# A two-layer hybrid block on one core: the second layer's compression issued earlier, the last layer norm on PSUM sums, the overflow branch behind the stores

## The chip, the cores and the metric

The kernel runs on one core of a Trainium2 chip. The metric is the device time of one execution in microseconds; three runs are given, and their median counts. The engines are called as in the profile: PE (TensorE matmuls), PEld (TensorE weight loads), DVE (VectorE), ACT (ScalarE), POOL (GpSimd), SP (SyncE, which here issues nearly all DMA transfers).

## The reference

256 tokens of width 1024 in float32 go through two layers. Layer 1 has a mixer of differential and sparse attention and a dense feed-forward net; layer 2 has a mixer of block attention and a compressed-and-selected attention (NSA), and a mixture of 8 experts with 2 experts for each token. Every part is followed by a layer norm of `alpha * x + part`:

```python
x = layer_norm(DN_ALPHA * x + mix, ln_mix_g[l], ln_mix_b[l])
ffn = moe_swiglu(x, w_router, b_router, w_gate, w_up, w_down)   # layer 2
x = layer_norm(DN_ALPHA * x + ffn, ln_ffn_g[l], ln_ffn_b[l])
```

The compression of NSA takes blocks of 32 tokens (stride 16), adds a position term, and puts each through a small net to get one compressed key and one value per block:

```python
h = moveaxis(blocks + pe, 3, 2).reshape(B, Nc, G, L * dh)
return gelu(h @ phi_w1) @ phi_w2
```

## The kernel before

**Stages.** Layer 1's attention runs until about 150 us, its feed-forward net until about 340, layer 2's attention until about 500, the experts until about 1366, and the last layer norm to the end. Products in float32 precision are made of three passes over split operands: ACT casts a weight tile `raw` to `wh`, DVE subtracts to get `wl` (lines 150 and 152), and PE multiplies (lines 164 to 166). All weight tiles are 128x1024 float32 (512 KB), loaded by SP in program order into a ring of `raw` tiles; a load waits until the tile's former content has been used.

**Layer 2's attention.** The projections of the normed input are made by `project()`, each from four weight tiles (three for the 280 columns of `c_w`): first kv (`c_kv`), then dq, then w, ckB, cq and cv. Names that come up below: `kvc`, the projected kv rows; `kp`, their regrouping on PE by 16 small products (L710); `km`, ACT's copy of it; `xr`, eight DVE copies into the order of the compression (L721); `hp`, 32 products with the eight phi tiles that SP loads (L729, L731); `cmp_hs`, DVE's copy of it; `ht`, the sum over four groups (L737); `cmp_u`, the gelu; `kc` and `vc`, the compressed keys and values. All of this is `compress()`, and stands in the program behind the w projection. `router_weights()` (L854 to L862) turns the layer norm's rows into the router's weights on PE (`rtps`, `rsps`), DVE and ACT (`rowT`, `gwr`) and stands ahead of the w projection. `compressed()` makes the scores against the compressed keys. The softmaxes are those of `softmax8` (L364 the mask product `sps`, L369 the maximum, L372 the exponentials `e`).

A scheduler moves instructions within each engine's order where it expects them to fit; in the experts PE's order is that of the program.

**Experts.** Each expert's 3584 columns are taken in chunks of 1024; experts with few tokens use 64 slots (`gate_up_small`, `down_small`): `pgu` (L1124), activation `h_s`, its transpose `tps` (L1151), the copy `hT_s`, and `y` (L1169). When an expert is done, `combine` scales `y` by the gate, splits it in two parts `yh` (ACT) and `yl` (DVE), multiplies both by the transposed dispatch matrix into a bank `cps` of PSUM (L1191, L1192), and DVE adds that bank to the sum `acc` (here named `x`) in SBUF (L1196), once for each of two token tiles t and two halves c.

**The end.** Slots can be too few for the tokens. A flag `overi` is therefore read by every engine (L1245), and each engine branches on it (L1249) over a long piece of code that computes such tokens. With these inputs the flag is zero and the piece is jumped over. Behind it stand the loads of the last layer norm's rows g and b (L224, L225, on SP), the statistics (L233), the reciprocal root (L206 to L214, for each of two token tiles with its own instructions), the normalising steps on DVE (L242, L244) for t=0 and on ACT, POOL and DVE for t=1 (L1265 to L1267), and four stores (L1269).

Of the kernel before, what the change touches and what calls it, by code (L numbers as in the profile page):

```python
# [8 lines left out]
F32 = mybir.dt.float32  # L9
F32R = mybir.dt.float32r  # L10
# [7 lines left out]
P = 128  # L18
S = 256
D = 1024  # L20
# [19 lines left out]
def hybrid_kernel(ctx, tc, x, ev_w_in, ev_w_out, dif_lambda, dif_subln, ffd_w_gate, ffd_w_up, ffd_w_down,  # L40
# [56 lines left out]
    colrow = const.tile([P, P], F32, name="colrow")  # L97
# [3 lines left out]
    identb = const.tile([P, P], BF16, name="identb")  # L101
    nc.vector.tensor_copy(identb, ident)
    causalb = const.tile([P, P], BF16, name="causalb")
    nc.vector.tensor_scalar(causalb, colrow, 0.0, NEG, op0=ALU.is_gt, op1=ALU.mult)

    loads = []
# [594 lines left out]
            nc.vector.tensor_tensor(fold[r], ident[r, q * 32:q * 32 + 30],  # L701
                                    ident[r, q * 32 + 30:q * 32 + 31].to_broadcast([32, 30]), ALU.add)

    def compress():
        kp = bank((P, 2, 2, P), "kp")
        for z in range(2):
            for g in range(2):
# [10 lines left out]
        for z in range(2):  # L718
            for g in range(2):
                for jj in range(2):  # L720
                    nc.vector.tensor_copy(  # L721
                        xr[:, z, 8 * jj:8 * jj + 8, g * NCMP:(g + 1) * NCMP],
                        km[:, z, g].rearrange("p (n j) -> p j n", j=8)[:, :, jj:jj + NCMP])
        hp = bank((P, 2, S), "hp")
        for z in range(2):
            for q in range(4):
# [178 lines left out]

    rbank = bank
    project(xp, w1[:, 2048:2560], 512, c_kv, None, (normed[-2],) * 3 + (normed[-1],))
    project(xp, w1[:, 1536:2048], 512, c_dq)
    router_weights()
    project(xp, w1[:, 2560:2840], 280, c_w)  # L910
    compress()
    ec = compressed()
    project(xp, w1[:, 512:1024], 512, c_rope(to_blocks, ckB, False))
    os_ = [nsa_start(qt) for qt in range(NT)]
    project(xp, w1[:, 0:512], 512, c_rope(to_heads, cqT, True))
    project(xp, w1[:, 1024:1536], 512, lambda t, ps: nc.scalar.copy(cv[:, t], ps))
# [78 lines left out]
    nc.vector.tensor_scalar(overi, over, 0.49, None, op0=ALU.add)  # L995

    acc = x3

    def columns(r):
        return (posm[:, :, 0:1], weight[:, :, 0:1]) if r is None else (posr[:, :, r:r + 1], weightr[:, :, r:r + 1])  # L1000
# [197 lines left out]
    def experts(runs, groups, small, disp):  # L1198

        turns, pend = [], []  # L1200

        def mid():
            while turns:
                turns.pop(0)()

        for p, (r, base) in enumerate(runs):
            if r is None:
                e = 0
            else:
                with behind(loads[-1] if p else None):  # L1210
                    e = nc.values_load(idxi[0:1, r:r + 1], engines=(mybir.EngineType.SP,), min_val=1, max_val=NE - 1)
            ws = weights_of(e)
            sm = r in small
            xe, gs, dT = disp.pop((r, base))
            ys = [yp.tile([P, 512], F32, tag="y", name="y") for _ in range(1 if sm else 2)]
            for i, (c0, n) in enumerate(CHUNKS):
                hs = (gate_up_small if sm else gate_up)(ws, c0, n, xe, mid)
                for f in pend:
                    f()
                ts = []  # L1220
                turns.append(lambda ts=ts, hs=hs, sm=sm: ts.extend((turn_small if sm else turn)(hs)))
                pend = [lambda ws=ws, c0=c0, n=n, ts=ts, ys=ys, sm=sm: (down_small if sm else down)(ws, c0, n, ts, ys)]
# [6 lines left out]
            pend.append(lambda ys=ys, gs=gs, dT=dT, p=p: turns.append(  # L1229
                lambda: combine(ys, gs, dT, p == 0 and bool(small))))  # L1230
        mid()
        for f in pend:
            f()
        mid()

    disp = dispatch_small(None, True)
    for t in range(NT):
# [2 lines left out]
        with tc.issue_after(marks["d"]):  # L1240
            nc.vector.tensor_tensor(xl[:, t], x3[:, t], xh[:, t].bitcast(F32), ALU.subtract)
    with products_in_order():
        experts([(r, 0) for r in ORDER], {0: ((1,),), 1: ((2, 4), (3,)), 3: ((5,), (6,)), 5: ((7,),)}, FEW, disp)
    def tokens_over(i):
        return nc.values_load(overi[0:1, i:i + 1], min_val=0, max_val=S)  # L1245

# [2 lines left out]
    with tc.If(any_over > 0):  # L1249
        for i, run in enumerate(MORE):  # L1250
            with tc.If(tokens_over(i + 1) > 0):
                experts([run], {}, (), dispatch([run]))

    g, b = ln_rows(1, 1, nc.sync, raw_tile)
    for t in (1, 0):
        z = acc[:, t]
        mu, r = layer_stats(z)
        cs = [slice(h * 512, (h + 1) * 512) for h in range(2)]
        if t == 0:
            normalize(z, mu, r, g, b, z)  # L1260
        else:
            mr = act.tile([P, 1], F32, tag="ln_mr", name="ln_mr", bufs=2)
            nc.vector.scalar_tensor_tensor(mr, mu, -1.0, r, op0=ALU.mult, op1=ALU.mult)  # L1263
            for c, eng in zip(cs, (nc.gpsimd, nc.vector)):
                nc.scalar.activation(z[:, c], z[:, c], AF.Identity, bias=mr, scale=r)  # L1265
                eng.tensor_tensor(z[:, c], z[:, c], g[:, c], ALU.mult)  # L1266
                eng.tensor_tensor(z[:, c], z[:, c], b[:, c], ALU.add)  # L1267
        for c in cs:
            nc.sync.dma_start(out[0, t * P:(t + 1) * P, c], z[:, c])  # L1269


_INS = ['x', 'ev_w_in', 'ev_w_out', 'dif_lambda', 'dif_subln', 'ffd_w_gate', 'ffd_w_up', 'ffd_w_down',
# [35 lines left out]
```

## Time and profile before

| | |
|---|---|
| three runs | 1387.89, 1393.18, 1397.38 us |
| median | 1393.18 us |
| profiled execution, its own time | 1393.63 us |
| its span in the profile | 1391.9 us |
| mean granted TensorE clock | 0.96 |
| PE busy | 1306.8 us (94%) |
| DVE busy | 753.0 us (54%) |
| ACT busy | 543.4 us (39%) |
| DMA, mean over the span | 309 GB/s |

Busy shares are means over stages that differ: in the experts' stage the DMA engines are busy nearly all the time, in the attention PE is, and at the end none is. Idle time counts only where nothing else runs on the engine that everything waits for. Rows of the trace follow below, in a section of their own.

### The profile page before, as it was taken

What the parts mean: (1) busy time and instruction counts of PE and PEld (TensorE: products, weight loads), DVE (VectorE), ACT (ScalarE), POOL (GpSimd) and SP (SyncE); (2) the same over time, 40 slices, a digit from 0 to 9 for tenths busy, and PEclk for the clock granted to TensorE, in tenths of its full rate; (3) what the DMA queues carried; (4) which work ended last, traced back from release to release, by engine and by line L of the source; (5) the groups of instructions that cost most, each with busy time, mean ns of one, the idle gap of its engine ahead of it and who ended that gap; (6) DMA issues with size and microseconds to landing.
All of it is one profiled execution on the core that took longest, in us unless ns stands there. A gap on an engine that the chain in (4) does not pass through costs nothing. (4 is left out here: it accounts for less than half of the span.)

```text
span 1391.9 us, 18210 instructions
## 1 busy us (share of the span) xinstructions
PE 1306.8 (94%) x6136; PEld 851.5 (61%) x6136; DVE 753.0 (54%) x1194; ACT 543.4 (39%) x796; POOL 48.9 (4%) x79
## 2 busy tenths in 40 slices
PE   8979999998988989998999999999999999999992
PEld 7856888886864763335367874546885436885430
DVE  6987755547578551111178963137994127894304
ACT  4464444432446310001066751135773025773100
POOL 2200000001220000000000000000000000000000
PEclk9999999999999979998999999899999999999996
DMA  9244646545553399899999999899999999999992
GB/s 351 73 136 137 227 144 219 182 122 164 175 153 121 126 358 401 340 409 409 402 409 408 402 409 403 320 408 409 407 405 380 409 401 409 409 402 409 408 402 99
DMA packets 146805, 429.98 MB, mean 309 GB/s; under 512 B 15696, under 2 KB 23280, under 8 KB 146704
## 3 DMA queue, kind: packets, MB, share of 16 engines
q1 hardware_dynamic: 146000, 426.48, 80.7%
q0 software_dynamic: 704, 2.26, 0.6%
q8 instruction: 50, 0.82, 0.2%
q14 instruction: 51, 0.42, 0.1%
HBM read 427.64 MB, written 1.05 MB: 308 GB/s over the span
## 5 line engine op out<-in xcount | busy, mean ns | idle before, releaser
L152 DVE TENSOR_TENSOR wl<-raw,wh 128x1024 fp32r<-128x1024 f32 x378 | 453.5, 1224 | 101.7 <-ACT wh L150 94.1
L150 ACT CAST wh<-raw 128x1024 fp32r<-128x1024 f32 x378 | 388.3, 1047 | 201.8 <-PE pg L166 48.7
L1124 PE MATMUL pgu<-raw,xs 128*64 128x512 f32 x1120 | 260.9, 614 | 0.0
L1124 PEld LDWEIGHTS pgu<-raw,xs 128*64 128x64 f32 x1120 | 80.9, 141 | 155.3 <-issue 141.9
L1169 PE MATMUL y<-raw,hT_s 128*64 128x512 f32 x560 | 127.6, 595 | 5.1 <-DMA raw<-in_moe_w_down_dram 3.5
L1132 DVE TENSOR_TENSOR h_s<-h_s,pgu 64x512 f32<-64x512 f32 x35 | 24.1, 690 | 177.8 <-ACT h_s L1131 177.7
L1131 ACT ACTIVATE h_s<-pgu 64x512 f32<-64x512 f32 x35 | 20.7, 590 | 187.0 <-PE pgu L1124 187.0
L1169 PEld LDWEIGHTS y<-raw,hT_s 128*64 128x64 f32 x560 | 38.6, 137 | 88.3 <-issue 67.2
L164 PE MATMUL mmps<-wh,xTh 128*128 128x512 f32 (+2 forms) x192 | 76.4, 399 | 1.0 <-ACT wh L150 0.8
L166 PE MATMUL mmps<-wh,xTl 128*128 128x512 f32 (+2 forms) x192 | 75.6, 395 | 1.8 <-DVE xTl L173 1.7
L165 PE MATMUL mmps<-wl,xTh 128*128 128x512 f32 (+2 forms) x192 | 74.2, 388 | 0.5 <-DVE wl L152 0.5
L164 PE MATMUL y<-wh,hTh 128*128 128x512 f32 x168 | 67.6, 402 | 5.0 <-ACT wh L150 5.0
L164 PE MATMUL pg<-wh,xeh 128*128 128x512 f32 x168 | 70.4, 419 | 0.4
L165 PE MATMUL pg<-wl,xeh 128*128 128x512 f32 x168 | 68.3, 407 | 2.3 <-DVE wl L152 2.3
L165 PE MATMUL y<-wl,hTh 128*128 128x512 f32 x168 | 67.4, 401 | 2.3 <-DVE wl L152 2.3
L166 PE MATMUL pg<-wh,xel 128*128 128x512 f32 x168 | 67.9, 404 | 0.0
L166 PE MATMUL y<-wh,hTl 128*128 128x512 f32 x168 | 67.2, 400 | 0.0
L166 PE MATMUL pu<-wh,xel 128*128 128x512 f32 x168 | 66.3, 395 | 0.0
L165 PE MATMUL pu<-wl,xeh 128*128 128x512 f32 x168 | 66.1, 394 | 0.0
L164 PE MATMUL pu<-wh,xeh 128*128 128x512 f32 x168 | 65.8, 392 | 0.0
L327 DVE COPY hT_s<-tps 128x256 f32<-128x256 f32 x18 | 7.6, 424 | 91.6 <-PE tps L1151 91.5
L325 ACT COPY hT_s<-tps 128x256 f32<-128x256 f32 x17 | 6.3, 372 | 114.6 <-PE tps L1151 114.6
(376 smaller groups left out, 1929.9 us busy)
## 6 DMA issues: line engine op xcount, KB each, us to landing
raw<-in_moe_w_up_dram SPq DMA_DIRECT2D x224, 512.0 KB, 10.1
raw<-in_moe_w_gate_dram SPq DMA_DIRECT2D x224, 512.0 KB, 10.1
raw<-in_moe_w_down_dram SPq DMA_DIRECT2D x224, 512.0 KB, 10.1
raw<-in_ffd_w_gate_dram SPq DMA_DIRECT2D x22, 512.0 KB, 4.9
raw<-in_ffd_w_up_dram SPq DMA_DIRECT2D x22, 512.0 KB, 4.5
raw<-in_ffd_w_down_dram SPq DMA_DIRECT2D x22, 512.0 KB, 4.8
raw<-in_ev_w_in_dram SPq DMA_DIRECT2D x20, 512.0 KB, 8.9
raw<-in_od_w_in_dram SPq DMA_DIRECT2D x20, 512.0 KB, 4.2
```

The source lines that it names most:

```text
L150: nc.scalar.copy(wh[:, :w], rv)
L152: nc.vector.tensor_tensor(wl[:, :w], rv, wh[:, :w].bitcast(F32), ALU.subtract)
L164: nc.tensor.matmul(ps, ah, wh, start=first and i == 0, stop=False)
L165: nc.tensor.matmul(ps, ah, wl, start=False, stop=False)
L166: nc.tensor.matmul(ps, al, wh, start=False, stop=last and i == n - 1)
L325: nc.scalar.copy(dst, src)
L327: nc.vector.tensor_copy(dst, src)
L1124: nc.tensor.matmul(p_[i * SMALL:(i + 1) * SMALL], xs[:, k0 + k], halves(w[k], n)[j], start=k0 + k == 0, stop=k0 + k == KD - 1)
L1131: nc.scalar.activation(h[:SMALL], p_[:SMALL], AF.Silu)
L1132: nc.vector.tensor_tensor(h[:SMALL], h[:SMALL], p_[SMALL:], ALU.mult)
L1169: nc.tensor.matmul(ys[0][i * SMALL:(i + 1) * SMALL], ts[k], w[:, i * 512:(i + 1) * 512], start=c0 == 0 and k == 0, stop=c0 + n == F_EXP an ...
```

## The change

It has three parts.

1. `compress()` is split. `compress_rows()` holds kp, km and xr and is called right behind the kv projection; `compress(xr)` holds the phi loads and all that follows and is called behind the dq projection, ahead of the w projection. `router_weights()` moves from ahead of the w projection to behind it, and `compressed()` from ahead of the ckB projection to behind it.
2. The last expert's combination is summed in PSUM. `residual()` splits the sum `acc` of the experts before into two parts `ah` and `al` and multiplies them by a unit matrix (`identr`) into four banks `zps` ahead of the last `y` products; `combine_last` adds the last expert to these banks. The last layer norm takes its statistics from the banks, has one reciprocal root of width 2 for both token tiles, normalises t=1 on ACT and DVE and t=0 on DVE, and GpSimd has no part in it. The loads of g and b stand behind the last weight load.
3. The branch on `overi` stands behind the four stores. If it is not jumped over, `acc` (copied back by ACT) is completed, normed and stored again.

Three small constants (`colrow`, `identb`, `causalb`) also move to a pool that is freed before the experts.

```diff
-    def compress():
+    def compress_rows():
         kp = bank((P, 2, 2, P), "kp")
...
+        return xr
+
+    def compress(xr):
         hp = bank((P, 2, S), "hp")
...
     project(xp, w1[:, 2048:2560], 512, c_kv, None, (normed[-2],) * 3 + (normed[-1],))
+    xr = compress_rows()
     project(xp, w1[:, 1536:2048], 512, c_dq)
+    compress(xr)
+    project(xp, w1[:, 2560:2840], 280, c_w)
     router_weights()
-    project(xp, w1[:, 2560:2840], 280, c_w)
-    compress()
+    project(xp, w1[:, 512:1024], 512, c_rope(to_blocks, ckB, False))
     ec = compressed()
-    project(xp, w1[:, 512:1024], 512, c_rope(to_blocks, ckB, False))
...
+    def residual():
+        zs = []
+        for t in range(NT):
+            ah = wsplit.tile([P, D], F32R, tag="wh", name="ah")
+            al = wsplit.tile([P, D], F32R, tag="wl", name="al")
+            nc.scalar.copy(ah, acc[:, t])
+            nc.vector.tensor_tensor(al, acc[:, t], ah.bitcast(F32), ALU.subtract)
+            zs.append([gu.tile([P, 512], F32, tag="gu", name="zps") for _ in range(2)])
+            for part in (ah, al):
+                for c in range(2):
+                    nc.tensor.matmul(zs[t][c], identr, part[:, c * 512:(c + 1) * 512], start=part is ah, stop=False)
+        return zs
+
+    def combine_last(zs, ys, gs, dT):
+        yh, yl = split_y(ys[0], gs)
+        for part in (yh, yl):
+            for t in (1, 0):
+                for c in range(2):
+                    rows = slice(c * SMALL, (c + 1) * SMALL)
+                    nc.tensor.matmul(zs[t][c], dT[rows, t], part[rows], start=False, stop=part is yl)
...
         mid()
+        zs = residual() if last else None
         for f in pend:
             f()
         mid()
+        if last:
+            combine_last(zs, ys, gs, dT)
+        return zs
...
+    g, b = ln_rows(1, 1, nc.sync, raw_tile)
+    x4 = [raw_tile() for _ in range(NT)]
...
+    for t in (1, 0):
+        for c in range(2):
+            nc.vector.bn_stats(st[:, t, c], zs[t][c])
+        nc.vector.bn_aggr(mv[:, t], st[:, t].rearrange("p a b -> p (a b)"))
+    r = rsqrt(mp, mv[:, :, 1], 1.0, EPS, NT)
+    mr = mp.tile([P, 1], F32, name="last_mr")
+    ready = nc.vector.scalar_tensor_tensor(mr, mv[:, 1, 0:1], -1.0, r[:, 1:2], op0=ALU.mult, op1=ALU.mult)
+    cs = [slice(c * 512, (c + 1) * 512) for c in range(2)]
+    for c in range(2):
+        nc.scalar.activation(x4[1][:, cs[c]], zs[1][c], AF.Identity, bias=mr, scale=r[:, 1:2])
+    with behind(ready.ins):
+        for c in range(2):
+            z = x4[0][:, cs[c]]
+            nc.vector.scalar_tensor_tensor(z, zs[0][c], mv[:, 0, 0:1], g[:, cs[c]], op0=ALU.subtract, op1=ALU.mult)
+            nc.vector.scalar_tensor_tensor(z, z, r[:, 0:1], b[:, cs[c]], op0=ALU.mult, op1=ALU.add)
+            nc.sync.dma_start(out[0, 0:P, cs[c]], z)
+
+    for t in range(NT):
+        for c in range(2):
+            nc.scalar.copy(acc[:, t, cs[c]], zs[t][c])
+    for c in range(2):
+        z = x4[1][:, cs[c]]
+        nc.vector.tensor_tensor(z, z, g[:, cs[c]], ALU.mult)
+        nc.vector.tensor_tensor(z, z, b[:, cs[c]], ALU.add)
+        nc.sync.dma_start(out[0, P:2 * P, cs[c]], z)
+
     def tokens_over(i):
...
-    g, b = ln_rows(1, 1, nc.sync, raw_tile)
-    for t in (1, 0):
-        z = acc[:, t]
-        mu, r = layer_stats(z)
...
+        g, b = ln_rows(1, 1, nc.sync, raw_tile)
+        for t in range(NT):
+            layer_norm(acc[:, t], g, b)
+            nc.sync.dma_start(out[0, t * P:(t + 1) * P], acc[:, t])
```

The first place is layer 2's attention, on SP. The listing is the order of DMA issues, minus for before and plus for after; `od_w_in` are the projections' weights, `nsa_phi_w` the phi tiles.

```order
 L131 DMA raw<-in_od_w_in_dram 128x2x512 x8
+L733 DMA raw<-in_nsa_phi_w_dram 128x4x256 x8
 L131 DMA raw<-in_od_w_in_dram 128x3x280 x2
 L131 DMA raw<-in_od_w_in_dram 128x2x280
-L729 DMA raw<-in_nsa_phi_w_dram 128x4x256 x8
-L131 DMA raw<-in_od_w_in_dram 128x2x512 x8
```

The eight phi loads now stand ahead of the three loads of the w projection, and the loads for ckB and cq still behind both.

The second place is PE in the same stage. Before, the rows around hp and ht, behind the products of the ckB projection, which the scheduler had put ahead of them:

```order
L165 MATMUL mmps<-wl,xTh 128x512
L166 MATMUL mmps<-wh,xTl 128x512
L731 MATMUL hp<-raw,xr 32x256 x32
L737 MATMUL ht<-fold,cmp_hs 128x30 x4
L164 MATMUL mmps<-wh,xTh 128x512
```

After the change, the rows around hp, at the end of the dq projection; `hps` are the transposes of dq's rows, and the products of 280 columns are those of w:

```order
L164 MATMUL mmps<-wh,xTh 128x512
L333 MATMUL hps<-ident,roped 128x128 x4
L165 MATMUL mmps<-wl,xTh 128x512
L166 MATMUL mmps<-wh,xTl 128x512
L735 MATMUL hp<-raw,xr 32x256 x5
L333 MATMUL hps<-ident,roped 128x128 x4
L735 MATMUL hp<-raw,xr 32x256 x12
L333 MATMUL hps<-ident,roped 128x128 x4
L735 MATMUL hp<-raw,xr 32x256 x15
L164 MATMUL mmps<-wh,xTh 128x280
```

hp and ht stood next to each other; now hp stands between dq and w, and ht (L741) inside the w projection.

The third place is the end of SP's order. Before, from the last weight load on; the code that the branch jumps over is left out:

```order
L131 DMA raw<-in_moe_w_down_dram 128x1024
L1245 TENSOR_LOAD overi
L1245 ISA x2
L1249 COMPARE_AND_BRANCH
...
L224 DMA raw<-in_ln_ffn_g_dram 128x1024
L225 DMA raw<-in_ln_ffn_b_dram 128x1024
L1269 DMA out_dram<-x_2897 128x512 x4
```

And after the change:

```order
L131 DMA raw<-in_moe_w_down_dram 128x1024
L1310 TENSOR_LOAD overi
L1310 ISA x2
L224 DMA raw<-in_ln_ffn_g_dram 128x1024
L225 DMA raw<-in_ln_ffn_b_dram 128x1024
L1298 DMA out_dram<-raw 128x512 x2
L1307 DMA out_dram<-raw 128x512 x2
L1314 COMPARE_AND_BRANCH
```

The loads of g and b no longer stand behind the branch, and the branch stands behind the stores.

## Rows read from the trace of the kernel before

**Rows 1.** Busy time by stretches of the span. Columns: stretch in us and its length; busy us and number of instructions of PE, PEld, DVE, ACT and POOL; granted TensorE clock (1.00 is full speed); busy share of the 16 DMA engines; GB/s.

```profile
340.00:500.00 160.00, 149.28 (x875) 110.90 (x875) 107.91 (x258) 67.78 (x169) 19.02 (x25) 1.00 0.53 176
500.00:520.00 20.00, 14.37 (x66) 10.56 (x66) 13.75 (x62) 4.43 (x6) 0.24 (x1) 0.58 0.85 338
...
800.00:1080.00 280.00, 271.12 (x1205) 173.87 (x1203) 153.22 (x160) 125.23 (x145) 0.00 (x0) 0.95 1.00 393
1080.00:1360.00 280.00, 270.16 (x1237) 151.32 (x1236) 131.48 (x136) 105.71 (x123) 0.00 (x0) 0.99 1.03 406
...
400.00:450.00 50.00, 46.06 (x221) 30.56 (x219) 42.87 (x94) 31.57 (x88) 6.89 (x5) 1.00 0.37 112
```

**Rows 2.** The order of events on PE in 384 to 397 us: start, length (of a group from its first start), engine, line, operation, out<-in, shape, count; in brackets the idle time ahead of it and what ended that.

```profile
385.69 0.39 PE L165 MATMUL mmps<-wl,xTh 128*128 128x512 f32 x1
385.92 0.39 PE L166 MATMUL mmps<-wh,xTl 128*128 128x512 f32 x1
388.46 3.66 PE L731 MATMUL hp<-raw,xr 128*32 128x256 f32 x64 [2.16 <-DVE xr L721]
395.17 1.05 PE L737 MATMUL ht<-fold,cmp_hs 128*128 128x30 f32 x8 [3.04 <-DVE cmp_hs L734]
```

**Rows 3.** The same for DVE (VectorE) in the same stretch.

```profile
387.80 1.51 DVE L721 COPY xr<-km 128x120 f32<-128x120 f32 x8
...
393.19 1.23 DVE L152 TENSOR_TENSOR wl<-raw,wh 128x1024 fp32r<-128x1024 f32 x1 [3.29 <-ACT wh L150]
394.34 0.68 DVE L734 COPY cmp_hs<-hp 128x512 f32<-128x512 f32 x1
```

**Rows 4.** PE's waits summed by what was waited for, 380 to 460 us: us in total, times, the longest.

```profile
PE sps L364 <- ACT e L372: 3.0, 3, 1.4
```

**Rows 5.** The order of events on all engines from 1360 us to the end of the span; SPq is SyncE's queue, and its rows are DMA issues.

```profile
1361.94 2.80 PE L1169 MATMUL y<-raw,hT_s 128*64 128x512 f32 x12 [0.52 <-DVE hT_s L327]
...
1365.64 1.08 PE L1169 MATMUL y<-raw,hT_s 128*64 128x512 f32 x4 [0.90 <-SPq L1249]
...
1368.89 1.29 DVE L1196 TENSOR_TENSOR x<-x,cps 128x512 f32<-128x512 f32 x2 [0.59 <-PE cps L1192]
...
1371.40 0.69 DVE L1196 TENSOR_TENSOR x<-x,cps 128x512 f32<-128x512 f32 x1 [0.31 <-PE cps L1192]
...
1375.30 2.47 DVE L233 BATCH_NORM_STATS2 ln_st<-x 128x6 f32<-128x512 f32 x4 [3.22 <-DVEq L1249]
...
1377.70 0.33 DVE L234 BATCH_NORM_AGGREGATE ln_mv<-ln_st 128x2 f32<-128x12 f32 x2
...
1379.67 1.41 DVE L242 SCALAR_TENSOR_TENSOR x<-x,ln_mv,raw 128x512 f32<-128x512 f32 x2 [1.40 <-DMA raw<-in_ln_ffn_g_dram]
...
1383.99 4.81 SPq L1269 DMA_DIRECT2D out_dram<-x  x4
1384.17 1.57 POOL L1266 TENSOR_TENSOR x<-x,raw 128x512 f32<-128x512 f32 x1 [881.96 <-ACT x L1265]
...
1386.33 1.63 DVE L1267 TENSOR_TENSOR x<-x,raw 128x512 f32<-128x512 f32 x1
```

**Rows 6.** One step of the chain that ended last: start, length, what.

```profile
1375.24 4.40 DMA raw<-in_ln_ffn_g_dram
```

**Rows 7.** SyncE's waits, 1365 us to the end.

```profile
SPq L224 <- DVEq L1249: 9.2, 1, 9.2
...
SPq L1304 <- DMA out_dram<-x: 1.4, 2, 0.8
```

**Rows 8.** The order of events on PE, 358 to 372 us.

```profile
363.12 0.38 PE L164 MATMUL mmps<-wh,xTh 128*128 128x280 f32 x1
...
371.66 0.39 PE L164 MATMUL mmps<-wh,xTh 128*128 128x512 f32 x1
```

**Rows 9.** The order of DMA issues on SyncE, 326 to 400 us: the start of the first, the time from the first to the last, the count.

```profile
335.79 17.37 SPq L729 DMA_DIRECT2D raw<-in_nsa_phi_w_dram  x8
359.84 28.43 SPq L131 DMA_DIRECT2D raw<-in_od_w_in_dram  x8
```

**Rows 10.** All instructions of line 729 (the phi loads): length in ns (smallest, median, largest), first and last start in us; and the time from issue to landing.

```profile
L729 SPq DMA_DIRECT2D raw<-in_nsa_phi_w_dram x8: 367/368/1253, 335.8 to 352.8; - x8
...
DMA to landing us min/median/max: 5.4/7.2/12.2
```

**Rows 11.** DVE's groups by line, 364 to 395 us: line, operation, out<-in, shapes, count; busy us in all, mean ns of one; idle time ahead.

```profile
L860 DVE TENSOR_TENSOR gwr<-wr,rowT 128x32 f32<-128x32 f32 x1 | 0.7, 723 | 0.0
...
L327 DVE COPY rowT<-rtps 128x512 f32<-128x512 f32 x1 | 0.7, 678 | 0.0
```

**Rows 12.** All instructions of line 217, one step of a reciprocal root of width 4 in layer 1: ns smallest, median, largest, first and last start in us.

```profile
L217 DVE TENSOR_TENSOR rsq_q<-rsq_q,rsq_m x6: 151/159/161, 102.2 to 116.9; 128x4 f32<-128x4 f32 x6
```

**Rows 13.** All instructions of line 1249, the branch on any tokens over the slots: the compare and the semaphore instructions that follow it on each engine, ns smallest, median, largest, first and last start in us.

```profile
L1249 SPq EVENT_SEMAPHORE  x9: 17/17/17, 1360.3 to 1365.7; - x9
L1249 ACTq EVENT_SEMAPHORE  x2: 17/17/17, 1369.8 to 1369.9; - x2
...
L1249 SPq COMPARE_BRANCH  x1: 53/53/53, 1355.1 to 1355.1; - x1
L1249 ACTq COMPARE_BRANCH  x1: 50/50/50, 1367.4 to 1367.4; - x1
L1249 PEldq COMPARE_BRANCH  x1: 3462/3462/3462, 1370.8 to 1370.8; - x1
```

More of the change, by code (lines that the diff above doesn't have):

```diff
@@ L95, in hybrid_kernel @@
     rt = fr.tile([P, NT, 5, 32], F32, name="rt")
-    colrow = const.tile([P, P], F32, name="colrow")
+    colrow = fr.tile([P, P], F32, name="colrow")
     nc.gpsimd.iota(colrow, pattern=[[1, P]], base=0, channel_multiplier=-1, allow_small_or_imprecise_dtypes=True)
@@ L100, in hybrid_kernel @@
     nc.vector.tensor_scalar(ident, colrow, 0.0, None, op0=ALU.is_equal)
-    identb = const.tile([P, P], BF16, name="identb")
+    identb = fr.tile([P, P], BF16, name="identb")
     nc.vector.tensor_copy(identb, ident)
-    causalb = const.tile([P, P], BF16, name="causalb")
+    causalb = fr.tile([P, P], BF16, name="causalb")
     nc.vector.tensor_scalar(causalb, colrow, 0.0, NEG, op0=ALU.is_gt, op1=ALU.mult)
@@ L997, in hybrid_kernel @@
     acc = x3
+    identr = mp.tile([P, P], F32R, name="identr")
+    nc.vector.tensor_copy(identr, ident)
     def columns(r):
@@ L1196, in combine, with experts @@
                     nc.vector.tensor_tensor(acc[:, t, cs], acc[:, t, cs], ps, ALU.add)
-    def experts(runs, groups, small, disp):
+    def residual():
[17 more added lines that the diff above has]
+                    nc.tensor.matmul(zs[t][c], dT[rows, t], part[rows], start=False, stop=part is yl)
+    def experts(runs, groups, small, disp, last=False):
         turns, pend = [], []
@@ L1228, in experts @@
                             disp.update(dispatch([runs[n_] for n_ in q]))
-            pend.append(lambda ys=ys, gs=gs, dT=dT, p=p: turns.append(
-                lambda: combine(ys, gs, dT, p == 0 and bool(small))))
+            if not (last and p == len(runs) - 1):
+                pend.append(lambda ys=ys, gs=gs, dT=dT, p=p: turns.append(
+                    lambda: combine(ys, gs, dT, p == 0 and bool(small))))
         mid()
+        zs = residual() if last else None
         for f in pend:
@@ L1242, in hybrid_kernel @@
     with products_in_order():
-        experts([(r, 0) for r in ORDER], {0: ((1,),), 1: ((2, 4), (3,)), 3: ((5,), (6,)), 5: ((7,),)}, FEW, disp)
+        zs = experts([(r, 0) for r in ORDER], {0: ((1,),), 1: ((2, 4), (3,)), 3: ((5,), (6,)), 5: ((7,),)}, FEW, disp, True)
+    g, b = ln_rows(1, 1, nc.sync, raw_tile)
+    x4 = [raw_tile() for _ in range(NT)]
+    st = mp.tile([P, NT, 2, 6], F32, name="last_st")
+    mv = mp.tile([P, NT, 2], F32, name="last_mv")
+    for t in (1, 0):
[22 more added lines that the diff above has]
+        nc.sync.dma_start(out[0, P:2 * P, cs[c]], z)
     def tokens_over(i):
@@ L1252, in hybrid_kernel @@
                 experts([run], {}, (), dispatch([run]))
-    g, b = ln_rows(1, 1, nc.sync, raw_tile)
-    for t in (1, 0):
-        z = acc[:, t]
-        mu, r = layer_stats(z)
[L1258 to L1269, printed above, removed]
+        g, b = ln_rows(1, 1, nc.sync, raw_tile)
+        for t in range(NT):
+            layer_norm(acc[:, t], g, b)
+            nc.sync.dma_start(out[0, t * P:(t + 1) * P], acc[:, t])
 _INS = ['x', 'ev_w_in', 'ev_w_out', 'dif_lambda', 'dif_subln', 'ffd_w_gate', 'ffd_w_up', 'ffd_w_down',
```

## The prediction

> **What bounds the kernel now.** I read the page first, then the table of windows, then the order of events in the two places that the change touches. From 520 us on, the mixture of experts is a stream of weights: DMA is busy 1.00 to 1.03 of the time and moves 393 to 406 GB/s until 1360 us [rows 1]. Nothing in the change shortens that stream. So a gain can come only from ahead of it (the stream's steady part starts when the first expert's products free tiles, and these wait for the second layer's attention) or from behind it. An earlier end of the attention moves the whole stream forward one for one, as long as the stream's own stops stay what they are: in 500 to 520 us the granted clock is 0.58 and DMA 0.85 [rows 1], a stop that starts with the experts and would move along.
>
> In the attention PE is the bound: 149 of 160 us busy [rows 1]. I looked for its holes. Two of them belong to the compression: 2.16 us ahead of the products hp, released by VectorE's copies xr, and 3.04 us ahead of ht, released by the copy cmp_hs [rows 2]. VectorE shows why: xr runs at 387.80, only after km, and cmp_hs at 394.34, behind a split wl that waited 3.29 us for its cast [rows 3]. The chain kp, km, xr, hp, cmp_hs, ht is serial, and PE has nothing else in its order meanwhile. Three smaller holes in the softmaxes (3.0 us) belong to ACT's exponentials [rows 4].
>
> Behind the stream the last product ends at 1365.64 + 1.08 = 1366.72, and the span at 1391.9: 25.2 us in which no engine is saturated. Reading down [rows 5]: combine until 1372.09, VectorE idle 3.22 us on its own branch, statistics at 1375.30, idle again until 1379.67 for the row of ln_ffn_g, last VectorE work 1386.33 + 1.63 = 1387.96. The load of that row took 4.40 us [rows 6] and was issued only after VectorE's branch: SP waited 9.2 us for it [rows 7].
>
> **The change, part by part.** *Compression.* kp, km and xr now stand behind the kv projection, inside the dq projection; hp behind dq, ht inside the w projection. Nothing is added: the same 32 hp products run (64 passes in 3.66 us). What matters is whether each input is there in time. Before, w's first product starts at 363.12 [rows 8], right behind dq's; kp comes in ahead of that and about as much of the router's products goes out, so hp can start near 362. xr's inputs are older: the kv projection ended long before, and kp stands beside dq's products. The phi tiles were issued from 335.79 on, over 17.37 us, behind the three w loads [rows 9]; now they are three loads sooner. The last was issued near 353 and the slowest landing was 12.2 us [rows 10], so 365 before and about 361 to 362 now: just in time, the tightest margin of this part. hp takes 3.66 us ahead of w, so the ckB projection, whose first product stood at 371.66 [rows 8], comes near 374. The loads of ckB and cq were issued from 359.84 over 28.43 us, the later ones only when hp freed the phi tiles from 388 on [rows 9]; now hp frees these tiles at 362 to 366, so no load of ckB comes later and those of cq come earlier. I therefore let both holes vanish: -5.2.
>
> Against that, the router's weights move behind the ckB projection. VectorE pays two copies of 0.68 and two products of 0.72 us [rows 11], 2.8 in all, in a stretch where it is already busy 42.87 of 50 us [rows 1]. Cover is the projections that remain there for PE; if it is gone, all of 2.8 shows. Most of these pieces stand between projections in the new order, so I take a quarter, +0.7. The w and ckB projections run earlier than the softmaxes want them as filler, but the value products of the first block of queries take that place in the new order; the holes of [rows 4] stay: zero, between 3.0 less (they close) and 3.5 more (as many again, and a bit). Attention: -4.5, between -8 (both holes and these close) and +1 (the 5.2 gained, and 2.8 and 3.5 lost again).
>
> *Seeding and combining.* Two casts and two subtractions of 128x1024 on ACT and VectorE stand far ahead, while both are idle. On PE eight products zps stand ahead of the last four y tiles: at the spacing of [rows 2] (0.23) 1.8 us. PE has just 0.52 and 0.90 us of waits there, but the last tile was awaited until 1365.64 anyway; I take +0.2 (bounds 0 and 1.8): products end at 1366.9. The combine then gives its first finished bank 2.2 us later, as L1196 started 2.17 after the product before [rows 5]: 1369.1. The four additions L1196 (2.7 us) are gone, as the statistics read the banks themselves. PSUM as a source costs nothing here: L1196 reads it in 0.69. Four statistics in 2.47 and two aggregates in 0.33 end at 1371.9. The reciprocal root is now one of width 2: 12 dependent steps of 0.16 [rows 12], which I take as 0.19 with the wait for the one before (0.16 to 0.30), 2.3; and 0.15 for mr: 1374.3. By then g and b, issued at about 1360 behind the last weights, have long landed. VectorE does four scalar-tensor-tensor and four tensor-tensor: before, two of the first took 1.42, and one of the second 0.69 alone (L1196) but 1.63 beside GpSimd's own [rows 5]. GpSimd has no part now, so 4 x 0.67 + 4 x 0.60 (their starts' spacing in pairs) = 5.1. ACT's two activations lie beside it. Last VectorE work T = 1379.4, against 1387.96.
>
> *The branch.* It stands behind the stores now, on SP also. Before, from T to the end 3.9 us passed: 0.84 to the end of the last issue at 1388.80 [rows 5], 1.4 waiting for landings [rows 7], 1.7 of final waits. Now SP branches first. On the rows, a branch holds VectorE for 3.22 [rows 5], ACT from 1367.4 to 1369.8, PE for 3.46, and SP itself from 1355.1 to 1360.3, while the last weights were moving [rows 13]. DMA is quiet at the end, so I take 3.1, near VectorE's and PE's (2.4 to 5.2), and 0.7 for SP's nine semaphore instructions behind it. The landing hides in that. End: T + 0.84 + 3.1 + 0.7 + 1.7 = 1385.7, against 1391.9: -6.2, between -7.0 and -4.1 by the branch's bounds, -2.5 with 1.6 more for zps. So the branch is no longer waited for by the layer norm, but by the end.
>
> [...]
>
> **Sum.** -4.5 - 6.2 = -10.7. The profiled execution took 1393.63 (1.7 around its span), so 1382.9. The median of the runs is 1393.18, 0.45 lower: 1382.5.
>
> **The rivals.** *Only the tail gains* (0.22): the two holes close, but PE meets the same wait later, in the softmaxes, where VectorE now has 2.8 us more. For it: VectorE's 42.87 of 50, and holes that ACT's exponentials already end. Against: the new order gives PE other work between them. -6.2: 1387. *More* (0.18): PE's holes in the softmaxes shrink too, because the compression's later VectorE steps leave that stretch, -3.5 (to -8), and a branch of 2.4 gives -0.7: 1378.3. *The branch costs next to nothing* (0.05): SP goes on at once, as if what stands behind the jump were at hand; the end then follows the landing of the last store, T + 3.9 as before: 1380.1. Against it stand [rows 13]. *Slower* (0.05): hp starves. It sits in PE's order ahead of the w projection, so a late phi tile stops everything behind it; SP's queue serves phi, w and ckB in turn, and w's loads now follow eight phi loads. Each us that the last phi tile lands after 362 costs one. Before, the slowest landed at 365, which would cost 3. It decides from a landing at 373 on (10.7 us lost): 1394 and more. Nothing in [rows 10] is that late. That the change does nothing is excluded: SP's wait of [rows 7] must go, as g is issued ahead of the work it waited for.
>
> **How the numbers follow.** My forecast has 0.50, with its own range of 1379 to 1387 (attention -2 to -7, tail -4.1 to -7.0, not both at an end). The bounds together reach from -15.0 to -3.1, 1378 to 1390; the runs of before lie 9.5 us apart, so I widen by 2 and 1: 1376 to 1391, leaving out the slow rival and the ends of the runs. A measurement of this kernel can tell about 1% (13.9 us) from no change. Faster than that means under 1379.2: six in ten of *more*, a quarter of *next to nothing*, a fifth of my forecast by scatter, some 0.22. Slower: 0.04. Within: 0.74.
>
> **What would show it.** PE without holes ahead of hp and ht, hp near 362 and ht within w; the last expert's stream ending about 4.5 earlier than 1365.6, near 1361. Then statistics some 2.2 us after the last product, no DMA wait ahead of the normalising steps, single VectorE steps of 0.6 to 0.75, and SP 3 us in its branch behind the last issue. I am wrong if the y products end at 1365 or later, if a hole of like size stands ahead of ckB's products or in the softmaxes, or if the end lies more than 7 us behind the last VectorE step.

## The result and the profile after

The changed kernel takes 1381.08 us (median of 20 runs), the kernel before 1389.22 (20 runs, 1385.44 to 1398.56). Of the changed kernel's runs, 19 lie at 1375.58 to 1387.49, and one, with 1500.79 us at a mean granted clock of 0.83, is left out of the comparison. The ratio is 0.9931, 95% interval 0.9917 to 0.9946: 9.6 us less, between 7.5 and 11.5 (the two medians lie 8.1 apart). Forecast were 1382.5 us and 10.7 less. The profiled execution of after took 1381.53 us (span 1379.4), that of before 1393.63: the latter lies 4.4 above the median of its 20 runs, so the 12.5 us between the two spans are more than the change is worth.

The windows of after, columns as in [rows 1]:

```profile
340.00:500.00 160.00, 152.60 (x873) 111.60 (x874) 108.35 (x260) 68.17 (x169) 17.44 (x24) 0.99 0.52 177
500.00:520.00 20.00, 14.35 (x70) 10.54 (x68) 13.85 (x63) 4.43 (x6) 0.24 (x1) 0.66 0.86 338
...
800.00:1080.00 280.00, 269.78 (x1204) 170.22 (x1202) 151.20 (x160) 122.55 (x142) 0.00 (x0) 0.96 1.00 396
1080.00:1360.00 280.00, 271.65 (x1242) 152.30 (x1244) 132.51 (x136) 107.23 (x123) 0.00 (x0) 0.99 1.02 402
```

The stream of weights is what it was: DMA at 1.00 to 1.02 of the time. In the attention PE is busy 3.3 us more of the same 160, so its idle time fell by as much; up to 1.7 of the 3.3 can be the same work at half clock (the granted clock is 0.99 here, and the last section shows the place). The order of events on PE there (it answers to [rows 2, 8]):

```profile
363.61 1.05 PE L735 MATMUL hp<-raw,xr 128*32 128x256 f32 x10
...
365.37 1.50 PE L735 MATMUL hp<-raw,xr 128*32 128x256 f32 x24
...
367.39 1.93 PE L735 MATMUL hp<-raw,xr 128*32 128x256 f32 x30
369.25 0.40 PE L164 MATMUL mmps<-wh,xTh 128*128 128x280 f32 x1
...
372.63 0.97 PE L741 MATMUL ht<-fold,cmp_hs 128*128 128x30 f32 x8
...
376.89 0.39 PE L164 MATMUL mmps<-wh,xTh 128*128 128x512 f32 x1
```

No row here has a bracket: PE waits neither ahead of hp nor of ht, and ht lies inside the w projection. PE's waits by what was waited for, 380 to 460 us (the answer to [rows 4]):

```profile
PE sps L364 <- ACT e L372: 3.2, 3, 2.1
PE oT L393 <- DVE pT L327: 1.3, 1, 1.3
PE ptps L387 <- ACT pT L325: 0.7, 1, 0.7
```

Before, that stretch had 2.2 + 3.0 (compression) + 3.0 + 0.9 = 9.1 us of waits on PE; now 5.2. The compression's are gone, and in this execution 1.3 us came back elsewhere. The tail in order of events (it answers to [rows 5]):

```profile
1355.32 0.73 PE L1216 MATMUL zps<-ah,identr 128*128 128x512 f32 x2
...
1357.38 3.65 PE L1176 MATMUL y<-raw,hT_s 128*64 128x512 f32 x16
...
1363.21 2.49 DVE L1285 BATCH_NORM_STATS2 last_st<-zps 128x6 f32<-128x512 f32 x4 [0.59 <-PE zps L1225]
1365.62 0.33 DVE L1286 BATCH_NORM_AGGREGATE last_mv<-last_st 128x2 f32<-128x12 f32 x2
...
1368.35 0.16 DVE L1289 SCALAR_TENSOR_TENSOR last_mr<-last_mv,rsq_y 128x1 f32<-128x1 f32 x1
1368.47 1.41 DVE L1296 SCALAR_TENSOR_TENSOR raw<-zps,last_mv,raw 128x512 f32<-128x512 f32 x2
...
1372.32 1.29 DVE L1306 TENSOR_TENSOR raw<-raw 128x512 f32<-128x512 f32 x2
1373.04 0.94 SPq L1307 DMA_DIRECT2D out_dram<-raw  x2
```

The last product ends at 1357.38 + 3.65 = 1361.03, statistics start 2.18 later, no wait for a DMA stands between, and VectorE ends at 1373.61, 12.58 behind the product (before: 21.24). From there to the end it is 5.79 us (before 3.94). SyncE's waits from 1373 us on show on what (the answer to [rows 7]):

```profile
SPq L1314 <- SPq L1314: 3.1, 1, 3.1
```

SyncE is in its own branch for 3.1 us. The profiled executions of all kernels below, in us, read from the order of events. "To pgu" is the time from PE's transpositions (tps) of layer 2's second tile of tokens, which begin 10.1 us behind those of the first in every execution, to the first expert product; "half clock" is what PE lost in that stretch up to 500 us, the sum of one minus the granted clock over stretches of 1 us. A stretch at half clock (granted 0.50) that begins at 500 to 508 us in every execution is left out: from the last product of the output projection (mops) to pgu all twelve take 17.12 to 17.15 us.

| kernel | to pgu | half clock | last y ends | VectorE ends behind it | end behind that | span |
|---|---|---|---|---|---|---|
| before | 174.58 | 0 | 1366.72 | 21.24 | 3.94 | 1391.9 |
| after | 174.19 | 1.7 | 1361.03 | 12.58 | 5.79 | 1379.4 |
| after, again | 174.54 | 3.4 | 1362.54 | 12.58 | 5.78 | 1380.9 |
| attention only | 173.42 | 0 | 1361.41 | 21.24 | 3.85 | 1386.5 |
| end only | 178.24 | 3.4 | 1364.20 | 12.57 | 5.93 | 1382.7 |
| no branch | 174.22 | 1.7 | 1359.32 | 12.58 | 3.30 | 1375.2 |
| short branch | 174.22 | 1.7 | 1360.77 | 12.56 | 3.27 | 1376.6 |
| casts later | 170.49 | 0 | 1356.85 | 12.58 | 5.87 | 1375.3 |
| old order, casts later | 175.04 | 1.7 | 1365.12 | 12.56 | 5.82 | 1383.5 |
| sums in SBUF | 174.91 | 1.7 | 1359.55 | 14.93 | 5.82 | 1380.3 |
| stores on GpSimd | 172.79 | 1.7 | 1356.35 | 12.57 | 4.88 | 1373.8 |
| both | 170.82 | 1.7 | 1355.76 | 12.58 | 5.06 | 1373.4 |

The two columns of the tail repeat to 0.03 and 0.2 us; the others do not. So the tail is read from one row, the attention needs several executions.

### The profile page after: what moved, and what is told of

The parts are those of the page before. It is cut to its first block, busy times and chain, and to the rows that moved or that the text cites. A ratio compares the mean times of both kernels' runs of the same rounds, so it can differ in the third digit from the quotient of the medians.

```text
span 1379.4 us, 18222 instructions
## 1 busy us (share of the span) xinstructions
PE 1305.4 (95%) x6144; PEld 849.9 (62%) x6144; DVE 752.0 (55%) x1189; ACT 548.1 (40%) x802; POOL 45.3 (3%) x77
## 3 DMA queue, kind: packets, MB, share of 16 engines
HBM read 427.64 MB, written 1.05 MB: 311 GB/s over the span
## 4 chain that ended last, share of the span: by engine, by line
PE 76%; DMA 12%; DVE 7%; ACT 2%; issue 2%; POOL 0%; SPq 0%; DVEq 0%; ACTq 0%; POOLq 0%
PE pgu L1131 14%; DMA raw<-in_moe_w_up_dram 6%; PE y L1176 5%; PE pg L164 4%; PE pu L164 4%; PE pu L166 4%; PE pu L165 4%; PE pg L165 4%; PE pg L166 4%; DMA raw<-in_moe_w_down_dram 3%; PE y L165 3%; PE y L166 3%; PE y L164 3%; PE mmps L165 2%; PE mmps L164 2%; PE mmps L166 2%
## 5 line engine op out<-in xcount | busy, mean ns | idle before, releaser
L173 DVE TENSOR_TENSOR hTl<-tps,hTh 128x512 fp32r<-128x512 f32 (+1 forms) x33 | 21.7, 671 | 56.1 <-ACT hTh L172 55.9
## 6 DMA issues: line engine op xcount, KB each, us to landing
raw<-in_moe_w_up_dram SPq DMA_DIRECT2D x224, 512.0 KB, 10.1
raw<-in_moe_w_gate_dram SPq DMA_DIRECT2D x224, 512.0 KB, 10.1
raw<-in_moe_w_down_dram SPq DMA_DIRECT2D x224, 512.0 KB, 10.1
```

Source lines behind the costliest of these rows:

```text
L173: lowed.append(nc.vector.tensor_tensor(lo, ps, hi.bitcast(F32), ALU.subtract).ins)
```

## The experiments

**Attention only.** Of the change, the new order of the compression (with the three constants' pool); the end as before.

```diff
 project(xp, w1[:, 2048:2560], 512, c_kv, None, ...)
+xr = compress_rows()
 project(xp, w1[:, 1536:2048], 512, c_dq)
-router_weights()
+compress(xr)
 project(xp, w1[:, 2560:2840], 280, c_w)
-compress()
-ec = compressed()
+router_weights()
 project(xp, w1[:, 512:1024], 512, c_rope(to_blocks, ckB, False))
+ec = compressed()
```

> The change's order of the second layer's attention, with the end of the kernel before. Theory A (the two holes of the compression close, but the projections that end 8 us earlier only meet ACT's casts of the output weights, which wait for their loads, so the experts start when they did before): no difference, within 2 us of before, first expert product pgu at 515 us, holes of 5 us in the softmaxes. Rival B (the prediction's term): 4.5 us faster, first pgu at 511.

Measured: 1387.49 us (12 runs) against 1390.57 (23 runs), ratio 0.9973 [0.9957, 0.9989]: 3.7 us less, 1.5 to 6.0. The attention's part is real, as the interval leaves out zero, and lies below the forecast of 4.5; both 4.5 and the 2 us that Theory A allows are inside the interval. The row lies between the two as well: pgu at 513.18, for 515 and 511 expected. The waits on PE from 380 to 460 us, 5.2 in all, are those of Theory A.

**End only.** The seeding, the combination and the end of the change, with the compression in its old place.

```diff
-xr = compress_rows()
...
-compress(xr)
...
+compress(compress_rows())
```

> The kernel before in the second layer's attention, with the change's end (seeded sums in PSUM, g and b early, branch behind the stores). Theory A: all of the change's gain, 6 to 7.5 us faster than before, from the last y product to the end 18.4 us in place of 25.2. Rival B: 6.2 us and so 2 to 4.5 us slower than the whole change.

Measured: 1384.66 us (12 runs), 0.9952 [0.9932, 0.9972]: 6.7 less (3.9 to 9.5), against a forecast of 6.2. The two parts add up: 3.7 + 6.7 = 10.4, with 9.6 for the whole. Both holes of the compression are there again in its order of events on PE, so they belong to the order and not to the constants' pool:

```profile
389.14 3.66 PE L735 MATMUL hp<-raw,xr 128*32 128x256 f32 x64 [2.51 <-DVE xr L722]
396.94 1.88 PE L741 MATMUL ht<-fold,cmp_hs 128*128 128x30 f32 x8 [4.14 <-DVE cmp_hs L738]
```

**No branch.** The whole change without the block behind the stores.

```diff
-    with behind(loads[-1]):
-        any_over = tokens_over(0)
-    with tc.If(any_over > 0):
-        ...
```

> The whole change without the branch on tokens over the slots and the code behind it (left out: the second pass for tokens that do not fit, none with these inputs). Theory A (SP's branch lies on the path behind the stores for about 3 us, and covers the landing): the end comes 1.5 to 2.5 us sooner after the last VectorE step, at 3.4 to 4.3 us behind it in place of 5.8. Rival (the landing and the final waits set the end, the branch is hidden): no difference from the whole change.

Measured: 1376.46 us (6 runs), 0.9887 [0.9861, 0.9914]. Behind VectorE's last step the end comes after 3.30 us instead of 5.79: the branch costs 2.5 us where it stands. SyncE's 3.1 us and the 0.6 of its nine semaphore instructions behind them stand where, without a branch, SyncE waits for landings:

```profile
SPq L1342 <- DMA out_dram<-raw: 1.4, 2, 0.8
```

The median lies 4.6 us below that of the change, more than the tail gives; in the profiled executions another 1.6 us lie in the stream.

**Short branch.** The branch stays, with its test and the second layer norm, and only the passes of the experts go from its body.

```diff
     with tc.If(any_over > 0):
-        for i, run in enumerate(MORE):
-            with tc.If(tokens_over(i + 1) > 0):
-                experts([run], {}, (), dispatch([run]))
```

> The whole change, with the flag, the branch and the second layer norm kept, but without the eight and one expert passes inside the branch (left out: the work for tokens over the slots, none here). Theory A (a branch costs what it costs because it jumps over some thousand instructions to code that has not been fetched; GpSimd, with few instructions to jump over, was past its branch in 0.2 us): the end comes 3.3 to 4.2 us behind the last VectorE step in place of 5.8, some 2 us faster than the whole change. Rival (a taken branch costs some 3 us in itself): 5.8 stays.

Measured: 1378.7 us (4 runs) against 1390.54 (11 runs), 0.9906 [0.9882, 0.9931]. The row decides: 3.27 us from VectorE's end to the end, as without a branch. All instructions of the branch's line on two engines in after (operation, count, ns smallest/median/largest, first and last start):

```profile
L1314 SPq EVENT_SEMAPHORE  x9: 17/17/17, 1377.1 to 1377.7; - x9
...
L1314 PEldq COMPARE_BRANCH  x1: 3465/3465/3465, 1363.3 to 1363.3; - x1
...
L1314 SPq COMPARE_BRANCH  x1: 53/53/53, 1374.0 to 1374.0; - x1
```

and with the short body:

```profile
L1314 SPq EVENT_SEMAPHORE  x4: 17/17/17, 1373.9 to 1374.2; - x4
...
L1314 PEldq COMPARE_BRANCH  x1: 223/223/223, 1363.0 to 1363.0; - x1
...
L1314 SPq COMPARE_BRANCH  x1: 53/53/53, 1373.7 to 1373.7; - x1
```

The comparison itself takes SyncE 53 ns in both. What follows it starts 3.1 us later behind the long body and 0.2 us later behind the short one; on PE the instruction shrinks from 3465 to 223 ns. So the price comes and goes with the body that is jumped over. What in the body sets it was not taken apart: the passes' own instructions, their semaphores and the branches inside went together, and that an engine waits for code not yet fetched, as Theory A has it, no view shows. The trace shows one thing more, the DMA queues that carry instructions. In after, from 1363 us to the end of the span, they move eight packets (number, MB, share of the 16 engines' time):

```profile
q14 instruction: 6, 0.05, 1.0%
q8 instruction: 2, 0.03, 0.9%
```

With the short body, and without a branch, the same stretch has none.

**Casts later.** The largest wait left on PE in the softmaxes of after (2.08 us) ends with an exponential on ScalarE. ScalarE's order of events there:

```profile
430.94 1.04 ACT L150 CAST wh<-raw 128x1024 fp32r<-128x1024 f32 x1 [2.17 <-DMA raw<-in_od_w_out_dram]
433.27 1.04 ACT L150 CAST wh<-raw 128x1024 fp32r<-128x1024 f32 x1 [1.28 <-DMA raw<-in_od_w_out_dram]
434.22 0.47 ACT L372 ACTIVATE e<-sps,nm 128x256 f32<-128x256 f32 x1
```

Two casts of the output weights wait for their DMA, and the exponential stands behind them in ScalarE's order. In this run the last two casts stand behind the exponentials.

```diff
-ws.append(split_w(raws))
+ws.append(split_w(raws, (), (None, None, exps[-1], exps[-1]) if late and c == 1 else ()))
```

> The whole change, with the casts of the last two output weight tiles put in ACT's order behind the last exponential of the NSA softmaxes. Theory A (these casts, waiting for DMA, hold up the exponentials and through them PE): PE's hole of 2.1 us near 435 goes, the experts start 1.5 to 3 us earlier than in the whole change, near 513. Rival (the softmax chain over VectorE and ACT is the bound itself): the hole comes back a little later, first pgu at 515, no difference.

Measured: 1380.44 us (6 runs), 0.9914 [0.9883, 0.9944]. The same exponential now waits for VectorE's maximum only, from 429.83 on, PE's wait of 2.08 is gone, and the way to pgu is 170.49 us against 172.5, the median of the seven executions with after's attention less what they lost at half clock:

```profile
429.83 0.47 ACT L375 ACTIVATE e<-sps,nm 128x256 f32<-128x256 f32 x1 [1.32 <-DVE nm L372]
```

The 170.49 lie below all seven of these (171.1 to 173.4). The time alone does not tell this run from after.

**Old order, casts later.** The same edit on the run "end only".

> The change's end with the attention's order of before, and the casts of the last two output weight tiles behind the last exponential of the NSA softmaxes. Theory A (these casts hold up the exponentials only in the changed order, where the projections' tiles come free later than the softmaxes begin to wait): within 1 us of the changed end alone, 6 to 7 us faster than before. Rival (they hold them up in both orders): 2 us faster than the changed end alone, 8 to 9 us faster than before.

Measured: 1384.32 us (6 runs), 0.9942 [0.9921, 0.9964], the time of "end only" within the error, as Theory A has it; 2 us less is not excluded either. The rows speak for the rival. PE's waits for exponentials, 3.0 us in "end only" and in before, are down:

```profile
PE sps L367 <- ACT e L375: 1.6, 3, 0.9
```

The way to pgu less half clock is 173.3, against 174.6 and 174.8 in the two executions with the old order. By this one execution the casts were in the way before, too, by some 1.3 us; but those with after's attention differ by 2.3 among themselves, so whether the casts cost more in the new order (about 2 us there) stays open.

**Sums in SBUF.** The last expert is combined as before, through additions into SBUF, and the statistics read SBUF; all else as in after.

```diff
-zs = experts([(r, 0) for r in ORDER], ..., FEW, disp, True)
+experts([(r, 0) for r in ORDER], ..., FEW, disp)
+zs = [[acc[:, t, c * 512:(c + 1) * 512] for c in range(2)] for t in range(NT)]
```

> The whole change, but the last expert is added to the sum in SBUF by VectorE as before (no seeding products, four additions), and the layer norm reads SBUF. Theory A (the PSUM sums save the additions on the path and cost 0.34 us of PE ahead of y): 2.5 to 3.3 us slower than the whole change, first statistics 5.4 us behind the last y product in place of 2.2, last y product 5.8 us behind the last transposes in place of 6.1. Rival (the additions overlap the statistics of the bank before): under 1 us slower.

Measured: 1381.6 us (6 runs), 0.9931 [0.9907, 0.9956], no difference from after by the time. By the rows VectorE ends 14.93 us behind the last product instead of 12.58 (2.35 more), but from the last transposition tps to the end of the products it is 5.17 us instead of 6.10, without the eight zps: 1.4 us in all. (Before has 5.76 there without zps, too; its last y tile waited 0.90 us [rows 5], the one here 0.20 for its weights.) That is half of what was expected: the statistics of the first tile start between the additions, 3.36 us behind the last product and not 5.4.

```profile
1361.71 1.28 DVE L1203 TENSOR_TENSOR x<-x,cps 128x512 f32<-128x512 f32 x2 [0.58 <-PE cps L1199]
...
1362.91 1.28 DVE L1286 BATCH_NORM_STATS2 last_st<-x 128x6 f32<-128x512 f32 x2
...
1364.11 1.27 DVE L1203 TENSOR_TENSOR x<-x,cps 128x512 f32<-128x512 f32 x2
```

**Stores on GpSimd.** The last two stores are issued by GpSimd, so that SyncE can take its branch earlier.

```diff
-        nc.sync.dma_start(out[0, P:2 * P, cs[c]], z)
+        nc.gpsimd.dma_start(out[0, P:2 * P, cs[c]], z)
```

> The whole change, with the last two stores issued by GpSimd's queue in place of SyncE's. Theory A (SyncE's branch is what the end waits for): SyncE branches 2 us earlier, the end comes 4.0 to 5.0 us behind the last VectorE step in place of 5.8, 1 to 1.8 us faster than the whole change. Rival (GpSimd's queue needs longer from issue to landing, and VectorE's own branch ends as late): no gain or up to 2 us slower.

Measured: 1378.26 us (6 runs), 0.9911 [0.9889, 0.9934]; 4.88 us from VectorE's end to the end, 0.9 less than after, which the row shows and the time alone does not. SyncE is still 2.9 us in its branch, but now the end waits for a landing again; GpSimd's issue of the last two takes 1.15 us against SyncE's 0.94:

```profile
SPq L1314 <- SPq L1314: 2.9, 1, 2.9
SPq L1356 <- DMA out_dram<-raw: 1.1, 1, 1.1
```

**Both, beside the change once more.** After with the last casts later and the last two stores on GpSimd, and after itself, on the same chip.

> The whole change with the casts of the last two output-weight tiles behind the exponentials (as in the run casts later) and the last two stores on GpSimd's queue (as in the run stores on GpSimd). If both gains are real and lie apart from each other, as one lies ahead of the stream of weights and the other behind it, the first expert's product pgu starts near 511.5, the last VectorE step lies 4.9 us ahead of the end, and the time is 2 to 5 us under that of the whole change in the same call: about 1377. Rival: the two single gains were scatter of the stream's stops; then the time lies within 1.5 us of the whole change's, with pgu still at 511 to 512, as what the attention gains is given back in the stream.

> The whole change once more, beside the run with both edits on the same chip. Both theories expect 0.993 of the kernel before, the median that it had, and a last VectorE step 5.8 us ahead of the end. If the first product pgu moves by some us against the 515.5 of the profile after while its order is the same, the half-clock spells of the attention are the cause, and the row of that stretch shows another place for them.

Measured: 1376.84 us (1375.33 to 1379.17, 6 runs), 0.9904 [0.9875, 0.9934], and for the change 1382.73 (1376.56 to 1386.88, 7 runs), 0.9934 [0.9904, 0.9963], against 1389.25 (12 runs). The gain over the change is 5.9 us by these medians and 4.2 by the 1381.08 above. All six runs lie at 1379.17 or lower, and of the 26 runs of the change that are compared ten do. The rows show 170.82 us to pgu and 5.06 at the end, near what was expected (pgu at 511.96 for 511.5; 4.9). PE's waits from 380 to 460 us are down to 2.5:

```profile
PE ptps L390 <- ACT pT L328: 1.5, 2, 0.7
PE sps L367 <- DVE nm L372: 0.7, 1, 0.7
PE ptps L390 <- DVE e L382: 0.3, 1, 0.3
```

So the version with both beats both kernels, and the rival is out. That each of the two gains has its part in it is shown by the rows; the times of the single runs don't show it. After itself repeats in the tail (5.78), but pgu starts at 514.80, only 0.7 us from 515.48, though PE lost 1.7 us more to half clock: the spells alone do not account for where pgu lands.

## Why the prediction came out as it did

**What bounds.** That a gain can come only from ahead of the stream or from behind it held: the parts measured alone add up to the whole. The claim that an earlier attention moves the stream one for one can't be read from one pair of executions: from pgu to the last product it took 851.3 us in before, 845.5 in after and 843.6 to 849.6 in the others, whichever order the attention had. In the two profiled executions pgu even starts at the same time (515.41 and 515.48), and 5.8 of their 12.5 us come out of the stream. So the last product's end near 1361, which the prediction gave as a sign of the attention's 4.5, came (1361.03) for another reason: luck. The 3.7 us of "attention only" agree with the claim, but no run tests it one for one.

**Compression.** Both holes closed, as forecast, with hp at 363.6 (forecast: near 362) and ht within w. The phi tiles were in time: their loads are issued from 332.80 to 348.8, with the longest landing 12.4 us, so by 361.2 at the latest (forecast: 361 to 362); VectorE has xr ready by 359.02 + 1.58 = 360.60. All instructions of the phi loads in after (the answer to [rows 10]):

```profile
L733 SPq DMA_DIRECT2D raw<-in_nsa_phi_w_dram x8: 367/1317/2195, 332.8 to 348.8; - x8
...
DMA to landing us min/median/max: 6.9/10.7/12.4
```

The rival in which hp starves is out. The router's weights cost PE no wait that its rows name.

The term was somewhat too large, -4.5 for -3.7 by the run "attention only", and the rows of PE give less still: less half clock, the way to pgu fell from 174.6 to values of 171.1 to 173.4 in seven executions, so by 1 to 3.5 us. Two steps of the prediction were off here. "The holes of [rows 4] stay: zero" was nearly right for the sum of the waits for exponentials (3.0 then, 3.2 to 3.6 in the seven), but one of the three is now 2.1 to 2.5 long, for 1.4. That is a hole of the size of the 2.16 ahead of hp, in the softmaxes, and so one of the signs that the prediction gave for being wrong. PE's other waits from 380 to 460 us rose from 0.9 to 2.0 in three of the seven executions; in the other four they are 0.7. ScalarE waited 3.4 us for output weights there, 2.4 before: the projections end some 8 us sooner, but the last four loads of output weights are issued only 2.4 sooner (425.91 for 428.26). The run "casts later" takes the largest of these waits away; that the rest comes from projections missing as filler was not tried. And "the same 32 hp products run (64 passes in 3.66 us)" was too cheap: in the new place they run in three pieces between transpositions, 1.05 + 1.50 + 1.93 = 4.48 us, and ckB's first product comes at 376.89 instead of near 374, also because hp starts 1.6 later than forecast. kp runs in three pieces, too: 0.34 + 0.56 + 0.80 = 1.70 us, where one of 1.15 stood before. What else PE's busy time grew by (161.2 of 173.4 us in "attention only", 159.1 of 174.6 before, so 2.1 in all) was not resolved further.

**Seeding and combining.** From the last tps to the end of the products it is 6.10 us for 5.76 before: +0.34, forecast +0.2 (against "sums in SBUF", 5.17, it is +0.93). The statistics start 2.18 behind (2.2), the root takes 2.4 with its waits (2.3), mr ends at 1368.51. T was forecast 12.5 behind the last product (1379.4 less 1366.9) and came 12.58 behind it. That PSUM as a source costs nothing held: L1285 takes 2.49 for four, [rows 5] has 2.47 from SBUF. That the sums in PSUM are worth much did not: 1.4 us of the tail's gain. The rest (g and b early, the branch out of the layer norm's way, one root for both tiles, VectorE without GpSimd beside it) was not taken apart.

**The branch.** SyncE was forecast 3.1 in it, and is; the end was forecast at T + 6.3 and came at T + 5.8, because the last issue ends 0.37 behind VectorE (0.84 before). The tail as a whole is 18.37 us behind the last product, for 25.18 before: -6.8, or -6.5 with the 0.34 for zps, forecast -6.2. The rival "next to nothing" (T + 3.9) is out in this kernel. Yet the run "short branch" comes near what it names: with little to jump over, what follows SyncE's comparison starts 0.2 us behind it in place of 3.1, and the end came at T + 3.3. Instruction transfers stand behind the branches of the long body (eight from 1363 us on, 0.08 MB) and none behind those of the short one. Whether an engine waits for any of them, no view shows.

**The sum.** -4.5 and -6.2 against -3.7 and -6.7 measured apart: -10.7 for -10.4 apart and -9.6 together. The forecast of the time, 1382.5, started from 1393.18, the median of three runs; with 20 runs the kernel before has 1389.22. By the ratio the forecast of the gain was 1.1 too large, by the medians (8.1) 2.6; with a start 4.0 too high the forecast of the time came out only 1.4 us from the result, which is in part luck.

## What to carry to other kernels

The branch, whose body was never entered here, still cost its jump, and that by the body (3.1 us over the long one, 0.2 over the short one, both on SyncE): look where the engines of such a branch are waited for, keep the long body away from the last instructions of the engine that ends the program, or let another queue issue the last stores (0.9 us here). When a hole on a bounding engine is closed, look at once for the next instruction that waits in order: here casts waiting for a DMA stood ahead of exponentials that were ready, and by PE's rows moving two of them gained about as much (2.0 us) as the moved compression (1 to 3.5). Read short tails from a row, but parts whose gain passes through a long stream of transfers from several executions.

## What the runs showed of the hardware

PE's granted clock fell to half (0.50 at 437 to 439 us in after) for short stretches in the attention, in some executions and not in others, with the same order of instructions: the way to pgu lost 1.7 us to it in after, 3.4 in the same kernel run again, and 3.4 in "end only", whose order there showed none in before. In after it stands at 436 to 440 us, right behind the wait of 2.08 us. The order of events on PE, and a window with columns as in [rows 1]:

```profile
435.28 0.27 PE L364 MATMUL sps<-causalb,identb 128*128 128x256 bf16 x1 [2.08 <-ACT e L372]
```

```profile
420.00:440.00 20.00, 16.61 (x63) 8.26 (x63) 15.06 (x33) 12.99 (x34) 0.00 (x0) 0.91 0.62 184
```

In before the waits of 2.16 and 3.04 us were followed by no such fall, in "end only" one stands at 395 to 402 us and begins inside the wait of 4.14 us (392.80 to 396.94). Nor does each one begin at a wait: in five executions with the new order (after again, no branch, short branch, stores on GpSimd, both) a fall begins at 419.6 to 423.1 us, where PE goes from one product to the next. In after, again, the same products of a projection take 0.63 us in place of 0.40:

```profile
417.99 1.95 PE L791 MATMUL cps<-kcB,dqT 128*128 128x30 f32 x16
...
420.10 0.40 PE L164 MATMUL mmps<-wh,xTh 128*128 128x512 f32 x1
...
421.23 0.63 PE L165 MATMUL mmps<-wl,xTh 128*128 128x512 f32 x1
```

After has these products in the same order from 419.11 us on, and no fall there. What decides it stays open. The loss is as large as what the attention's change gains, and is why one profile can't size it.

The stream differs in the same way. From pgu to the last product, summed as in the table, PE lost 31.5 us to half clock in before and 32.9 in "old order, casts later", the two longest (851.3 and 849.6 us), and 20.2 to 26.9 in the other ten (843.6 to 848.2). Whether the clock makes the stream longer, or the stream's stops make the clock fall, these rows don't tell.

GpSimd issued a store in 0.57 us (SyncE 0.33), and yet the end came 0.9 us sooner behind VectorE (4.88 for 5.79): SyncE, 2.9 us in its branch, no longer had the last two stores to issue.
